# Layer 1 of a two-layer decoder trunk on one Trainium2 core: tokens 14 to 1039 in tiles of 256, down products of 512 columns in four banks, output stores of 128 rows

## The chip, the core and the metric

The kernel runs on one core of one Trainium2 chip as a single launch. The metric is device microseconds. Of the kernel before there are three timed runs, with a median of 3075.25 us (3072.14 to 3075.53), and one profiled execution.

## What is computed

The trunk has two layers. Sixteen learned meta tokens stand ahead of 1024 tokens of 1024 features (1040 in all); the meta tokens are dropped at the end. Layer 0 is a Mamba-2 mixer and a gated feed-forward network with a causal convolution of three taps; layer 1 is an attention over a shared K and V and such a network again. All is float32. The change lies in layer 1 behind the attention:

```python
h = h + o @ sb_w_o[j]                                    # o: (1040, 1024)
h = h + _conv_ffn(_rmsnorm(h, ffn_norm[1]), ffn_w_up[1], ffn_conv_w[1], ffn_conv_b[1], ffn_w_down[1])
return _rmsnorm(h, final_norm)[:, N_META:]               # the last 1024 rows

def _conv_ffn(u, w_up, conv_w, conv_b, w_down):
    h = _causal_dwconv(u @ w_up, conv_w, conv_b)         # 3 taps: a token needs the two ahead of it
    g, val = jnp.split(h, 2, axis=-1)                    # D_FF = 2816 each
    return (jax.nn.silu(g) * val) @ w_down
```

## The kernel before, in words

Data lie transposed: 128 features on the partitions, tokens in the columns, so the stream h is 8 tiles of 128 x 1040. Every large product is made of three float32r matmuls (`mm3`, L153 to L155): each operand is split into a high part (made by ScalarE, ACT) and the rest (made by VectorE, DVE, for activations and by GpSimd, POOL, for weights); high times high, high times low and low times high are summed in one PSUM bank. A bank holds 128 x 512 float32, and there are eight: `mm` 2, `sm` 3, `lg` 2, `ex` 1.

Behind the attention, both layers use the same functions, with token tiles of FN = 260 columns (four of them, 1040 in all):

- `o_proj` loads the attention's output by pairs of heads and the stream h, and adds the output projection to h in PSUM (`accumulate`: DVE adds the bank into h at L378). `enter_ffn` adds the last two or four pairs, makes the sums of squares (`square_row`, L794) and the RMS factors, stores h to DRAM (`hm`), and `forms` makes the operands of the up projection.
- `up` is the up projection as a fast 2 x 2 matrix product with seven products in place of eight, over two groups of two tiles. The matmuls are 262 columns wide (260 and the two ahead that the convolution needs): 3696 of them. DVE and ACT make the convolution; each result of 128 x 260 is stored to DRAM (`g`, L887).
- `down` is the down projection, a fast product with seven products (order 1, 7, 6, 5, 3, 4, 2), over the first 16 of 22 row blocks in two rounds. Each product of a round has two **halves** (sets x = 0 and 1 of rows), so there are 2 x 7 x 2 = 28 halves. `operands` makes a half's operands: differences of weights on POOL (L974 to L983), of activations on DVE (L975 to L985, 1040 columns), the splits on ACT (L989, L991), POOL (L990, `wl`) and DVE (L992, `gl`). A half has 48 matmuls of 260 columns: 4 row groups f, 2 tiles t of 260, 2 row blocks, 3 matmuls. A product's sum lives in eight banks, one for each (t, f): half 0 opens them, half 1 closes them, and `add` (L1035 on ACT, L1037 on DVE) brings each into its accumulator. The next product's first half can open a bank only when the add of this product's has emptied it. Then six row blocks are left, done directly (`accumulate`, 576 matmuls of 260 columns) for one token tile after the other, while DVE sums the seven products (`sums`, L1008).
- `finish` follows each tile of 348 tokens (348, 348, 344) as soon as its columns are done: the final norm, a transposition in chunks of 116 tokens (112 for the last) on TensorE (PE), the scaling, and stores of 116 rows of 4 KB (L1444). The third tile's 344 tokens come behind the last matmul. There the squares are taken from the transposed banks: ACT does L1430, DVE copies and squares (L1426, L1428), and the results are scaled by DVE (L1442) and by ACT and POOL together (L1439, L1440).

The queues of ACT, DVE, POOL, SP (DMA issue) and PE are in order. Outside of the mixer and the attention, the scheduler of the tile framework sets the order by its own estimate of times, so a change of shapes can reorder an engine's work. Up to the last instruction of the attention, the changed kernel has the same instructions in the same order on PE, DVE (but for one memset), ACT, POOL and SP.

Of the kernel before, what the change touches and what calls it, by code (L numbers as in the profile page):

```python
# [13 lines left out]
P = 128  # L14
D = 1024
# [14 lines left out]
FN = 260  # L30
HB = 2
FW = 264

# [33 lines left out]
class Trunk:  # L67
# [99 lines left out]
    def split_half(self, t, s):  # L167

        x = self.Q(s, F32R)
        hi, lo = x[:, : L // 2], x[:, QW // 2 : QW // 2 + L // 2]  # L170
# [200 lines left out]
    def accumulate(self, h, f, s0, n, w, ks, front=0, bank=None, base=0):  # L371

        ps = (bank or (self.ex if f % 3 == 2 else self.mm))("acc")
        c, o = slice(s0 - base, s0 - base + n), slice(front + s0, front + s0 + n)
# [328 lines left out]
    def out_proj(self, hd, ys, yd, pool):  # L703
# [3 lines left out]
        for g in range(3):  # L707
            ops = [self.split(ys[g][q] if yd[g] is None else self.fetch(yd[g][q], "y"), "y") for q in range(4)]
            for f in range(KD):
                w = self.load_w(a["w_out_f"][g, f], 4 * P)  # L710
                if g == 0:
                    h[f] = self.fetch(hd[f], "h", front=HB)
                for s0, n in TT:
                    self.accumulate(h, f, s0, n, lambda i, f: (w[0][:, i * P : i * P + P], w[1][:, i * P : i * P + P]), ops, HB)
        ops = [[self.split_half(ys[3][q][:, L // 2 * x : L // 2 * (x + 1)], "y") for q in range(4)] for x in range(2)]
        ws = [self.load_wd(a["w_out"][12 + i], pool if i < 2 else None) for i in range(4)]
        return self.enter_ffn(0, h, [(ws, o) for o in ops], pool)
# [4 lines left out]
    def enter_ffn(self, layer, h, last, pool):  # L722


        nc = self.nc
        r = self.rp.tile([P, QW], F32, tag="r", name=self.nm("r"))
        nc.gpsimd.tensor_copy(r[:, :HB], self.zero[:, :HB])
        d = self.dp.tile([KD, P, L], F32, tag=f"hm{layer}", name=f"hm{layer}")
# [3 lines left out]
        def tile(j, work):  # L732
            ws, ops = last[j // 2]
            ms[j] = self.sm("ms")
            for f in range(KD):
                self.accumulate(h, f, FN * j, FN, lambda i, f: (ws[i][0][:, f * P : f * P + P], ws[i][1][:, f * P : f * P + P]), ops, HB, next(banks), L // 2 * (j // 2))
                self.square_row(ms[j], h, j, f)
# [3 lines left out]
        def factors(j):  # L741

            c = r[:, HB + FN * j : HB + FN * j + FN]
            b, ps = self.tmp("y")[:, :FN], ms.pop(j)[:, :FN]
# [9 lines left out]
        def rest():  # L754
            forms.append(form_tiles())
            yield from self.forms(h, r, 1, f"ffn_norm{layer}", forms[1][1:], pool)

        def form_tiles():
# [3 lines left out]
            for x in wide[1]:  # L762
                nc.gpsimd.memset(x.bitcast(F32)[:, HB + 2 * FN : 2 * FW], 0.0)
            own = {i: (self.Q("bh", F32R), self.Q("bl", F32R)) for i in (0, 2, 3, 4, 6)}
            out = {i: [tuple(x[:, k * FW : k * FW + HB + FN] for x in own[i]) for k in range(KD // 2)] for i in own}
            both = [tuple(x[:, k % 2 * 2 * FW : k % 2 * 2 * FW + HB + 2 * FN] for x in wide[k // 2]) for k in range(KD // 2)]
            out[1] = [tuple(x[:, : HB + FN] for x in hl) for hl in both]
            out[5] = [tuple(x[:, FN :] for x in hl) for hl in both]
            return out, out, both

        def store(x):
            for k in range(KD):
                nc.sync.dma_start(d[k, :, L // 2 * x : L // 2 * (x + 1)], h[k][:, HB + L // 2 * x : HB + L // 2 * (x + 1)])
# [7 lines left out]
        work = self.forms(h, r, 0, f"ffn_norm{layer}", forms[0][1:], pool)  # L781
# [8 lines left out]
    def square_row(self, ms, h, j, f):  # L790

        q = self.tmp("sq")[:, :FN]
        self.nc.scalar.activation(q, h[f][:, HB + FN * j : HB + FN * j + FN], AF.Square)
        self.nc.tensor.matmul(ms[:, :FN], self.ones, q, start=f == 0, stop=f == KD - 1, skip_group_check=True)  # L794
# [5 lines left out]
    def forms(self, h, r, t, gain, tiles, pool):  # L800


        nc = self.nc
        N, N2 = HB + FN, HB + 2 * FN
        tt = nc.vector.tensor_tensor
        out, both = tiles
        s = slice(2 * FN * t, 2 * FN * t + N2)

        new = slice(s.start + HB * t, s.stop)
        for k in range(KD // 2):  # L810
# [8 lines left out]
            b11, b12, b21, b22 = b1[:, :N], b1[:, FN:], b2[:, :N], b2[:, FN:]  # L819
# [39 lines left out]
    def up(self, layer, w0, forms, rest, pool):  # L859

        nc = self.nc
        tt = nc.vector.tensor_tensor
        N = HB + FN
        cw, cb = f"ffn_conv_w{layer}", f"ffn_conv_b{layer}"
        d = self.dp.tile([KF, P, L], F32, tag=f"g{layer}", name=f"g{layer}")

        def block(b, t, w):
# [10 lines left out]
            def conv(x, i, c):  # L878
                o = self.tmp("c")
                self.conv(x, o[:, :FN], FN, 3, HB, lambda q: self.par(cw, (KF * i + b) * 3 + q), self.par(cb, KF * i + b))  # L880
                if i == 0:
                    nc.scalar.activation(o[:, :FN], o[:, :FN], AF.Silu)  # L882
                return o

            def done(g, v, j):
                self.last_up = tt(g[:, :FN], g[:, :FN], v[:, :FN], op=ALU.mult)  # L886
                nc.sync.dma_start(d[b, :, FN * j : FN * j + FN], g[:, :FN])  # L887
# [44 lines left out]
    def down(self, layer, gd, hd, pool, after):  # L932
# [3 lines left out]
        nc, a = self.nc, self.a  # L936
        H, S = D // 2, L // 2
# [94 lines left out]
        def add(i, f, t, ps, first):  # L1032
            x = acc[i, f][:, FN * t : FN * t + FN]
            if first and i in (1, 5, 6, 7):
                nc.scalar.activation(x, ps[:, :FN], AF.Copy)  # L1035
            else:
                tt(x, x, ps[:, :FN], op=ADD)  # L1037
# [35 lines left out]
        for m in range(0, len(plan), 2):  # L1073
# [3 lines left out]
            if r == 0 and i == 7:  # L1077
                for f in range(KD):
                    nc.sync.dma_start(h[f][:, :L] if f < 4 else h[f][:, half(0)], hd[f] if f < 4 else hd[f, :, half(0)])
# [5 lines left out]
            for x in range(2):  # L1085
# [446 lines left out]
```

## Time and profile before

| | |
|---|---|
| three timed runs, median | 3075.25 us |
| profiled execution, first to last instruction | 3077.5 us |
| attention's end, start of `o_proj` on PE | about 2207 us |
| up projection on PE | 2311.7 to 2785.9 us |
| 28 halves of the down products on PE | 2786.0 to 2975.2 us |
| six direct row blocks, with the finish of two tiles between | 2975.2 to 3051.9 us |
| from there to the end | 25.6 us |

The profiled execution is 2.25 us (0.07%) above the median of the runs. In the page, busy time is summed by engine; PE counts a matmul from its start to its modelled end, so matmuls overlap, and the pace is read from start to start. "PEld" is the loading of weights, which runs beside. A row of the view by lines or of the timeline has engine, source line, operation, output <- inputs, shapes and count; in brackets stands the idle time of the engine before it and what ended that.

### The profile page before, as it was taken

To read this page: it belongs to the slowest core of one execution; us is meant where nothing else is said; L and a number is where in the kernel's file an instruction comes from. 1 tells how busy PE (TensorE), PEld (TensorE's weight loads), DVE (VectorE), ACT (ScalarE), POOL (GpSimd) and SP (SyncE) were. 2 spreads that over 40 slices of the span, in tenths; PEclk is the share of its full clock that TensorE was granted. 3 is DMA by queue.
4 is the path that set the end of the run, shared out by engine and by line. 5 is a ranking of instruction groups with operands and counts; after the bars stand their busy time and mean duration, and the time that the engine had idled before them with its cause. 6 is when DMAs were issued, how large, how long until landed. Compare 5 with 4: busy or idle time off the path is not lost.

```text
span 3077.5 us, 58674 instructions
## 1 busy us (share of the span) xinstructions
PE 2897.7 (94%) x22535; PEld 2782.2 (90%) x22535; DVE 2336.0 (76%) x4030; ACT 1645.5 (53%) x3403; POOL 1411.6 (46%) x1289
## 2 busy tenths in 40 slices
PE   5999999989998999998999999999897999998997
PEld 2999898879988999998999999999797999998996
DVE  3576868885369888778966888888759888888874
ACT  2555545553245555654334888777635555554332
POOL 1154435452335666657733222222225666666741
PEclk8999999999999999999999999999998999999998
DMA  3333323323221222244132222221431222225221
GB/s 110 108 93 93 105 88 109 101 71 138 70 83 56 83 77 75 80 136 152 47 122 77 64 60 67 62 57 48 140 112 59 80 84 77 76 86 179 76 97 55
DMA packets 123220, 273.41 MB, mean 89 GB/s; under 512 B 13468, under 2 KB 53020, under 8 KB 122940
## 3 DMA queue, kind: packets, MB, share of 16 engines
q1 hardware_dynamic: 117622, 258.54, 26.9%
q10 hardware_dynamic: 4054, 6.56, 0.6%
q8 instruction: 177, 2.90, 0.4%
q0 software_dynamic: 1264, 4.57, 0.4%
q14 instruction: 103, 0.84, 0.1%
HBM read 201.25 MB, written 53.45 MB: 83 GB/s over the span
## 4 chain that ended last, share of the span: by engine, by line
PE 67%; DVE 17%; ACT 5%; issue 5%; DMA 3%; POOL 2%; ACTq 0%; POOLq 0%; SPq 0%; DVEq 0%
PE p L153 9%; PE p L154 9%; PE p L155 9%; PE acc L153 5%; PE acc L154 5%; PE acc L155 5%; PE pj L153 5%; PE pj L154 5%; PE pj L155 5%; DVE gl L992 3%; PE po L1297 2%; PE lg L1255 2%; DMA x<-in_x 1%; PE wT L1282 1%; DVE D L573 1%
## 5 line engine op out<-in xcount | busy, mean ns | idle before, releaser
L153 PE MATMUL pj<-uh,wh 128*128 128x348 f32 (+2 forms) x1536 | 507.0, 330 | 16.1 <-DVE qs L1206 7.2
L154 PE MATMUL pj<-ul,wh 128*128 128x348 f32 (+2 forms) x1536 | 497.3, 324 | 0.0
L155 PE MATMUL pj<-uh,wl 128*128 128x348 f32 (+2 forms) x1536 | 495.6, 323 | 0.0
L154 PE MATMUL p<-bl,fh 128*128 128x262 f32 x1408 | 400.9, 285 | 14.1 <-DVE bl L814 14.1
L153 PE MATMUL p<-bh,fh 128*128 128x262 f32 x1408 | 402.1, 286 | 2.5 <-ACT fh L845 1.4
L155 PE MATMUL p<-bh,fl 128*128 128x262 f32 x1408 | 400.1, 285 | 0.0
L846 POOL TENSOR_TENSOR fl<-x,fh 128x1024 fp32r<-128x1024 f32 x88 | 212.5, 2416 | 353.3 <-ACT fh L845 275.4
L147 POOL TENSOR_TENSOR wl<-w,wh 128x1024 fp32r<-128x1024 f32 (+2 forms) x80 | 163.9, 2051 | 351.8 <-ACT wh L146 351.7
L153 PEld LDWEIGHTS pj<-uh,wh 128*128 128x128 f32 x1536 | 291.8, 190 | 23.7 <-DVE qs L1206 9.2
L154 PE MATMUL p<-bl,wh 128*128 128x262 f32 x1056 | 303.1, 287 | 8.7 <-DVE bl L814 8.7
L153 PE MATMUL p<-bh,wh 128*128 128x262 f32 x1056 | 302.3, 287 | 6.2 <-ACT bh L813 6.2
L155 PE MATMUL p<-bh,wl 128*128 128x262 f32 x1056 | 301.2, 286 | 0.0
L154 PEld LDWEIGHTS pj<-ul,wh 128*128 128x128 f32 x1536 | 292.0, 190 | 1.2 <-issue 0.5
L155 PEld LDWEIGHTS pj<-uh,wl 128*128 128x128 f32 x1536 | 291.4, 190 | 0.5 <-issue 0.2
L278 DVE SCALAR_TENSOR_TENSOR c<-p,params,c 128x260 f32<-128x260 f32 x528 | 251.4, 484 | 47.2 <-ACT c L275 37.5
L153 PE MATMUL acc<-gh,wh 128*128 128x260 f32 x896 | 262.1, 293 | 22.9 <-DVE p L1037 10.7
L154 PEld LDWEIGHTS p<-bl,fh 128*128 128x128 f32 x1408 | 267.2, 190 | 16.3 <-DVE bl L814 16.0
L153 PEld LDWEIGHTS p<-bh,fh 128*128 128x128 f32 x1408 | 266.8, 190 | 5.2 <-ACT bh L813 2.0
L154 PE MATMUL acc<-gl,wh 128*128 128x260 f32 x896 | 260.3, 291 | 9.8 <-DVE gl L992 9.5
L155 PEld LDWEIGHTS p<-bh,fl 128*128 128x128 f32 x1408 | 266.6, 190 | 0.1
L886 DVE TENSOR_TENSOR c<-c,c 128x260 f32<-128x260 f32 x176 | 255.7, 1453 | 7.5 <-ACT c L882 4.5
L155 PE MATMUL acc<-gh,wl 128*128 128x260 f32 x896 | 259.0, 290 | 1.2 <-POOL wl L990 1.2
(311 smaller groups left out, 8566.7 us busy)
## 6 DMA issues: line engine op xcount, KB each, us to landing
w<-in_w_up SPq DMA_DIRECT2D x88, 512.0 KB
g<-c SPq DMA_DIRECT2D x176, 130.0 KB
w<-in_w_down SPq DMA_DIRECT2D x44, 512.0 KB
w<-in_w_in SPq DMA_DIRECT2D x40, 512.0 KB
b<-g SPq DMA_DIRECT2D x32, 520.0 KB
E<-ea_d SPq DMA_DIRECT2D x32, 464.0 KB
D<-acs_d SPq DMA_DIRECT2D x32, 420.5 KB
h<-h_d SPq DMA_DIRECT2D x16, 520.0 KB
```

The costliest lines, as they stand in the source:

```text
L147: nc.gpsimd.tensor_tensor(wl[:, :n], w32[:, :n], wh[:, :n].bitcast(F32), op=ALU.subtract)
L153: mm(out, wh, uh, start=first, stop=False, skip_group_check=joins)
L154: mm(out, wh, ul, start=False, stop=False, skip_group_check=joins)
L155: mm(out, wl, uh, start=False, stop=last, skip_group_check=joins)
L278: nc.vector.scalar_tensor_tensor(out, ps[:, o + i : o + i + n], wcol(i), out, op0=ALU.mult, op1=ALU.add)
L573: nc.vector.tensor_scalar(dk[:, i], dk[:, i], self.cols[:n, 1, cc, h0 + i : h0 + i + 1], 0.0, op0=ALU.subtract, op1=ALU.min)
L846: tt(lo[:, :n], t, hi[:, :n].bitcast(F32), op=ALU.subtract)
L886: self.last_up = tt(g[:, :FN], g[:, :FN], v[:, :FN], op=ALU.mult)
L992: tt(gl, x, gh.bitcast(F32), op=SUB)
L1255: nc.tensor.matmul(ps[:nt, :m], part[:, c0 : c0 + nt], ks[a][:, s0 : s0 + m], start=x == 0, stop=x == 1)
L1282: nc.tensor.transpose(pt[:ns, x * CB : x * CB + nt], bt[a][:nt, x * CB : x * CB + ns], self.ident[:nt, :nt])
L1297: nc.tensor.matmul(po[64 * a : 64 * a + 64, w], v[: CH[c][1], c, 64 * a : 64 * a + 64], wt[a][: CH[c][1], c, :nt], start=x == 0, stop=x == ...
```

## The change

For layer 1 alone (FNS = 260 for layer 0, 256 for layer 1), and without any change in what layer 0 does:

- h is loaded from token 14 on (ORG = META - HB = 14): 1026 columns, two for the convolution and 1024 for the output. Tiles are 256 wide, the first of `o_proj` 258; the up matmuls are 258 wide, and all the DVE, ACT and DMA work of a tile shrinks from 260 to 256 columns.
- In `down` a half's columns are S = 512. Since that fits a bank, `parts` is one part of 512 columns: a half is 24 matmuls of 512 columns (4 f, 2 row blocks, 3 matmuls) into four banks, with adds of 512 columns. `kinds` becomes a cycle over eight banks, so that consecutive products take different fours.
- `finish` works on four tiles of 256 tokens in chunks of 128: two tiles behind the second direct tile, one behind the third, and one, the last, behind the fourth. Stores are of 128 rows; for the last tile they go out in halves of 512 columns, and all of its scaling is on DVE (L1466 of the changed kernel) in place of DVE, ACT and POOL.

```diff
-FN = 260
+FNS = (260, 256)
 HB = 2
+ORG = META - HB
...
     def enter_ffn(self, layer, h, last, pool):
-        nc = self.nc
+        nc, F = self.nc, FNS[layer]
...
+        edges = [0] + [HB + F * j for j in range(1, 5)]
+        if layer == 0:
+            edges[0] = HB
+            nc.gpsimd.tensor_copy(r[:, :HB], self.zero[:, :HB])
+        tiles = [(x, y - x) for x, y in zip(edges, edges[1:])]
...
     def down(self, layer, gd, hd, pool, after):
-        H, S = D // 2, L // 2
+        H, S = D // 2, 2 * F
+        parts = [(0, S)] if S <= 512 else [(0, F), (F, F)]
...
-        kinds = (self.mm, self.sm, self.lg, self.sm, self.mm, self.sm, self.lg, self.ex)
+        kinds = cycle((self.mm, self.sm, self.lg, self.sm, self.mm, self.sm, self.lg, self.ex))
...
+            o, n = parts[t]
             for q in range(2):
-                c, e = slice(q * H + f * P, q * H + f * P + P), slice(FN * t, FN * t + FN)
-                self.mm3(ps[:, :FN], wh[:, c], wl[:, c], gh[:, q, e], gl[:, q, e], first and q == 0, not first and q == 1)
+                c, e = slice(q * H + f * P, q * H + f * P + P), slice(o, o + n)
+                self.mm3(ps[:, :n], wh[:, c], wl[:, c], gh[:, q, e], gl[:, q, e], first and q == 0, not first and q == 1)
...
-                tt(x, x, ps[:, :FN], op=ADD)
+                tt(x, x, ps[:, :n], op=ADD)
...
-                for n, (t, f) in enumerate((t, f) for t in range(2) for f in range(4)):
+                for t, f in ((t, f) for t in range(len(parts)) for f in range(4)):
                     if x == 0:
-                        ps[t, f] = kinds[n]("acc")
+                        ps[t, f] = next(kinds)("acc")
                     part(ps[t, f], made[m + x], f, t, x == 0)
...
     def o_proj(self, hd, od, pool):
...
-            h[f] = self.fetch(hd[f], "h", front=HB)
+            h[f] = self.Q("h")
+            self.nc.sync.dma_start(h[f][:, : L - ORG], hd[f, :, ORG:])
             for j in range(4):
-                self.accumulate(h, f, FN * j, FN, lambda i, f: (w[0][:, i * P : i * P + P], w[1][:, i * P : i * P + P]), ops[j // 2], HB)
+                o, e = (HB + F * j) * (j > 0), HB + F * (j + 1)
+                self.accumulate(h, f, o, e - o, lambda i, f: (w[0][:, i * P : i * P + P], w[1][:, i * P : i * P + P]), ops[j // 2])
...
     def finish(self, h, j):
+        for i in ((0, 1), (2,), (3,))[j]:
+            self.finish_tile(h, i)
+
+    def finish_tile(self, h, j):
...
-        s0, n = TT[j]
-        chunks = [(i, *CH[3 * j + i]) for i in range(3)]
+        n = FNS[1]
+        s0, last = n * j, j == 3
+        chunks = [(i, s0 + P * i) for i in range(n // P)]
...
-                if b and i < 2:
-                    nc.scalar.activation(y[:m, w], p[:m], AF.Copy, scale=r[:m, i : i + 1])
-                    nc.gpsimd.tensor_tensor(y[:m, w], y[:m, w], self.gfin[:m, w], op=ALU.mult)
+                if b and not last:
+                    nc.scalar.activation(y[:, w], p, AF.Copy, scale=r[:, i : i + 1])
+                    nc.gpsimd.tensor_tensor(y[:, w], y[:, w], self.gfin[:, w], op=ALU.mult)
                 else:
-                    nc.vector.scalar_tensor_tensor(y[:m, w], p[:m], r[:m, i : i + 1], self.gfin[:m, w], op0=ALU.mult, op1=ALU.mult)
-            s = META if t0 == 0 else 0
-            nc.sync.dma_start(out[t0 + s - META : t0 + m - META, :], y[s:m, :])
+                    nc.vector.scalar_tensor_tensor(y[:, w], p, r[:, i : i + 1], self.gfin[:, w], op0=ALU.mult, op1=ALU.mult)
+                if last:
+                    nc.sync.dma_start(out[t0 : t0 + P, w], y[:, w])
+            if not last:
+                nc.sync.dma_start(out[t0 : t0 + P, :], y)
```

How this moves instructions is shown at three places. First DVE in the second round of the down products, from the low split of product 6's first half (`gl`, L992, L1001 in the changed kernel) to the last add of product 7 (`p` is its accumulator, `acc` the banks, `b` the activations); before:

```order
L992 TENSOR_TENSOR gl_34608<-b_33803,gh_34607 128x2x520
L985 TENSOR_TENSOR b_33803<-b_34219,b_33803 128x2x520
L1037 TENSOR_TENSOR p_33447<-p_33447,acc_34549 128x260
L1037 TENSOR_TENSOR p_33447<-p_33447,acc_34556 128x260
L992 TENSOR_TENSOR gl_34674<-b_33873,gh_34673 128x2x520
L1037 TENSOR_TENSOR p_33448<-p_33448,acc_34563 128x260
L1037 TENSOR_TENSOR p_33448<-p_33448,acc_34570 128x260
L985 TENSOR_TENSOR b_33873<-b_34287,b_33873 128x2x520
L1037 TENSOR_TENSOR p_33447<-p_33447,acc_34577 128x260
L1037 TENSOR_TENSOR p_33447<-p_33447,acc_34584 128x260
L1037 TENSOR_TENSOR p_33448<-p_33448,acc_34591 128x260
L1037 TENSOR_TENSOR p_33448<-p_33448,acc_34598 128x260
```

and now:

```order
L1001 TENSOR_TENSOR gl_34123<-b_33654,gh_34122 128x2x512
L994 TENSOR_TENSOR b_33654<-b_33902,b_33654 128x2x512
L1048 TENSOR_TENSOR p_33438<-p_33438,acc_34092 128x512
L1001 TENSOR_TENSOR gl_34161<-b_33696,gh_34160 128x2x512
L1048 TENSOR_TENSOR p_33438<-p_33438,acc_34099 128x512
L994 TENSOR_TENSOR b_33696<-b_33942,b_33696 128x2x512
L1048 TENSOR_TENSOR p_33439<-p_33439,acc_34106 128x512
L1048 TENSOR_TENSOR p_33439<-p_33439,acc_34113 128x512
```

Among the same operand steps (2 x 520 or 2 x 512 columns) stood eight adds of 260 columns from eight banks; four adds of 512 columns stand there now.

Second, POOL at the same place, from the weights' low part `wl` of product 7's first half to that of product 5's first half; before:

```order
L990 TENSOR_TENSOR wl_34478<-w_33944,wh_34477 128x1024
L977 TENSOR_TENSOR w_33944<-w_34082,w_33944 128x1024
L980 TENSOR_TENSOR w_33805<-w_33805,w_33944 128x1024
L990 TENSOR_TENSOR wl_34544<-w_34013,wh_34543 128x1024
L977 TENSOR_TENSOR w_34013<-w_34151,w_34013 128x1024
L990 TENSOR_TENSOR wl_34610<-w_33944,wh_34609 128x1024
L980 TENSOR_TENSOR w_33875<-w_33875,w_34013 128x1024
L983 TENSOR_TENSOR w_33944<-w_34217,w_33944 128x1024
L990 TENSOR_TENSOR wl_34676<-w_34013,wh_34675 128x1024
L983 TENSOR_TENSOR w_34013<-w_34285,w_34013 128x1024
L990 TENSOR_TENSOR wl_34742<-w_33805,wh_34741 128x1024
```

and now:

```order
L999 TENSOR_TENSOR wl_34049<-w_33739,wh_34048 128x1024
L986 TENSOR_TENSOR w_33739<-w_33821,w_33739 128x1024
L989 TENSOR_TENSOR w_33656<-w_33656,w_33739 128x1024
L999 TENSOR_TENSOR wl_34087<-w_33780,wh_34086 128x1024
L986 TENSOR_TENSOR w_33780<-w_33862,w_33780 128x1024
L999 TENSOR_TENSOR wl_34125<-w_33739,wh_34124 128x1024
L989 TENSOR_TENSOR w_33698<-w_33698,w_33780 128x1024
L992 TENSOR_TENSOR w_33739<-w_33900,w_33739 128x1024
L999 TENSOR_TENSOR wl_34163<-w_33780,wh_34162 128x1024
L999 TENSOR_TENSOR wl_34201<-w_33656,wh_34200 128x1024
L992 TENSOR_TENSOR w_33780<-w_33940,w_33780 128x1024
```

The shapes are the same. One difference of weights for product 3 (L983, now L992), which stood between the last two `wl`, has moved behind them.

Third, SP's last issues, the stores of the output; before:

```order
L1444 DMA out<-y_35794 100x1024
L1444 DMA out<-y_35824 116x1024
L1444 DMA out<-y_35809 116x1024
L1444 DMA out<-y_36043 116x1024
L1444 DMA out<-y_36073 116x1024
L1444 DMA out<-y_36058 116x1024
L1444 DMA out<-y_36309 116x1024
L1444 DMA out<-y_36319 112x1024
L1444 DMA out<-y_36314 116x1024
```

and now:

```order
L1470 DMA out<-y_34999 128x1024
L1470 DMA out<-y_35014 128x1024
L1470 DMA out<-y_35068 128x1024
L1470 DMA out<-y_35083 128x1024
L1470 DMA out<-y_35301 128x1024
L1470 DMA out<-y_35316 128x1024
L1468 DMA out<-y_35536 128x512 x2
L1468 DMA out<-y_35541 128x512 x2
```

Nine stores of 100 to 116 rows became six of 128 full rows and four of 128 half rows; behind the last matmul come the last three of before and the last four of now.

More of the change, by code (lines that the diff above doesn't have):

```diff
@@ L741, in factors @@
         def factors(j):
[L743 to L744 removed]
+            o, n = tiles[j]
+            c = r[:, o : o + n]
+            b, ps = self.tmp("y")[:, :n], ms.pop(j)[:, :n]
             if j % 2 == 0:
@@ L1434, in finish @@
+            nc.vector.tensor_tensor(ss[:, :2], s2[:, 0], s2[:, 1], op=ALU.add)
+            r = self.token_rstd(ss, P, 2)
+        for i, t0 in chunks:
             y = self.Q("y")[:, :D]
```

135 lines of the change are left out of this document (69 added, 66 removed).

## The prediction, before the changed kernel was run

> **What bounds the kernel now.** I read the page first, then the part behind the attention by stages (the changed kernel has the same program up to there), then the pace of matmuls by width, the waits of the down products, and the end. The stages are cut at 2834.4, 2881.1 and 2918.5 us where halves 6, 14 and 20 of the down products start on PE (counted by 48 matmuls from 2786.0):
>
> ```profile
> span 3077.5 us, 58674 instructions
> PE 67%; DVE 17%; ACT 5%; issue 5%; DMA 3%; POOL 2%; ACTq 0%; POOLq 0%; SPq 0%; DVEq 0%
> ```
>
> ```profile
> core 0: us, PE busy (x) PEld busy (x) DVE busy (x) ACT busy (x) POOL busy (x), PEclk, DMA share, GB/s
> 2203.00:2311.70 108.70, 108.50 (x857) 105.68 (x858) 58.64 (x131) 42.04 (x87) 26.71 (x19) 0.98 0.36 123
> 2311.70:2786.00 474.30, 458.46 (x3713) 454.33 (x3712) 396.86 (x633) 273.02 (x565) 304.08 (x173) 0.98 0.26 86
> 2786.00:2834.40 48.40, 39.68 (x291) 38.45 (x289) 45.27 (x22) 22.48 (x39) 41.06 (x14) 0.89 0.31 110
> 2834.40:2881.10 46.70, 46.53 (x384) 46.12 (x385) 32.91 (x33) 18.36 (x25) 27.27 (x11) 1.00 0.52 171
> 2881.10:2918.50 37.40, 35.05 (x291) 34.63 (x290) 36.19 (x34) 13.11 (x13) 35.82 (x12) 1.00 0.00 1
> 2918.50:2975.20 56.70, 51.35 (x386) 50.52 (x385) 43.24 (x64) 21.24 (x24) 32.42 (x12) 0.91 0.37 122
> 2975.20:3051.90 76.70, 76.70 (x650) 76.70 (x649) 39.94 (x84) 17.34 (x31) 11.59 (x9) 1.00 0.14 45
> 3051.90:3077.50 25.60, 3.00 (x26) 2.51 (x24) 7.95 (x20) 5.09 (x11) 3.05 (x2) 0.66 0.24 75
> ```
>
> PE sets the output projection, the up projection, halves 6 to 13 and the direct blocks: it is busy all through. In halves 0 to 5 and 14 to 19 DVE and POOL are both busy nearly without a gap, and PE is not. In halves 20 to 27 nobody is full: PE waits, and its clock (0.91) falls. The last 25.6 us hold almost no work.
>
> **Pace by width.** Operands and weights change with every matmul, so PE runs at a fixed step for each width. The timeline of PE has two runs without a break, 478 matmuls of 260 columns between the first pair of rows and 68 of 348 between the second (the rows that end them are the next instruction's):
>
> ```profile
> 2215.21 0.28 PE L154 MATMUL acc<-ol,wh 128*128 128x260 f32 x1
> 2272.56 0.38 PE L794 MATMUL ms<-sq,ones 128*128 128x260 f32 x1
> ...
> 1656.87 0.32 PE L153 MATMUL pj<-uh,wh 128*128 128x348 f32 x1
> 1667.65 0.32 PE L155 MATMUL pj<-uh,wl 128*128 128x348 f32 x1
> ```
>
> 57.35 us / 478 is 120.0 ns, 10.78 / 68 is 158.5 ns: 0.44 ns for each column. By that line 256 columns take 118.2, 258 take 119.1 against 120.9 for 262, and 512 columns 230.9; I take 230. No float32r matmul wider than 352 is in the trace, so this is bounded. Above: in proportion to 260 columns, 236 ns. Below: plain float32 matmuls of 512 columns, whose two records stand 1.02 - 0.59 = 0.43 us apart in the rows here (timeline, and the view of the tile S); if a record is two passes, one pass is 215 ns.
>
> ```profile
> 165.97 1.02 PE L619 MATMUL S<-xde,bk 116*128 116x512 f32 x2
> ```
>
> ```profile
> L619 PE MATMUL S<-xde,bk x64: 589/592/697, 166.0 to 674.0; 116*128 116x512 f32 x64
> L626 DVE TENSOR_TENSOR state<-state,S x28: 668/677/690, 182.9 to 681.4; 128x512 f32<-128x512 f32 x28
> ```
>
> The Trainium skill, "TensorE: Matmul & The Clock Gate", section "Back-to-back issue gap", gives the isolated gap as columns / 2.4 + 2.5 ns. At 260 columns that would be 110.8, and the trace has 120.0, so it does not hold here; at 512 it says 215.8, and by it the sum below would be 16 x 24 x 14.2 ns = 5.5 us better.
>
> **The waits of the down products.** PE's groups in 2786.0 to 2975.2:
>
> ```profile
> L153 PE MATMUL acc<-gh,wh 128*128 128x260 f32 x448 | 131.2, 293 | 10.9 <-DVE p L1037 5.3 <-DVE c L278 3.1 <-DVE h L1037 2.4
> L154 PE MATMUL acc<-gl,wh 128*128 128x260 f32 x448 | 130.5, 291 | 4.9 <-DVE gl L992 4.8
> L155 PE MATMUL acc<-gh,wl 128*128 128x260 f32 x448 | 130.0, 291 | 0.8 <-POOL wl L990 0.8
> ```
>
> 7.7 us are waits for a bank that DVE had still to empty (L1037), 4.8 for `gl`. A wait costs more than itself. Behind one of these waits, at 2928, the step is
>
> ```profile
> 2928.57 0.42 PE L154 MATMUL acc<-gl,wh 128*128 128x260 f32 x1
> 2928.79 0.42 PE L155 MATMUL acc<-gh,wl 128*128 128x260 f32 x1
> ```
>
> 0.22 us in place of 0.12: half clock, which the stage's 0.91 reflects. The adds are late because DVE's other work is slow, as its timeline and POOL's show:
>
> ```profile
> 2804.19 3.43 DVE L978 TENSOR_TENSOR b<-b,b 128x1040 f32<-128x1040 f32 x1
> 2857.79 1.23 DVE L992 TENSOR_TENSOR gl<-b,gh 128x1040 fp32r<-128x1040 f32 x1
> 2895.88 1.42 DVE L1037 TENSOR_TENSOR p<-p,acc 128x260 f32<-128x260 f32 x4
> ...
> 2882.36 2.40 POOL L990 TENSOR_TENSOR wl<-w,wh 128x1024 fp32r<-128x1024 f32 x1 [3.32 <-ACT wh L989]
> 2884.84 3.29 POOL L977 TENSOR_TENSOR w<-w,w 128x1024 f32<-128x1024 f32 x1
> 2914.96 6.76 POOL L990 TENSOR_TENSOR wl<-w,wh 128x1024 fp32r<-128x1024 f32 x2
> ```
>
> The same DVE step takes 1.2 us alone and 3.4 while POOL works, and POOL's goes from 2.4 to 3.3: about 1.2 + 2.2, they take turns. An add out of a bank (1.42 / 4, overlapping starts) stays at 0.35 to 0.42 in the midst of it. So a wider add is cheap, but operands cannot come faster than one DVE and one POOL step in 3.35 us.
>
> **The change part by part** (gains in us, against the profiled 3077.5).
>
> *Narrower tiles ahead of the products.* Output projection: 768 matmuls x 1.7 ns = 1.3, at least 0 if loads set it. Up projection: 3696 x 1.8 ns = 6.5; PE waits only at its start, on DVE, whose work shrinks by 1.5% too. Least 4, if DVE sets more of it. The shorter DMAs (1024 bytes in place of 1040) are hidden by PE; DMA is 26% busy in the up stage.
>
> *Halves 0 to 5* (48.4): the turns of DVE and POOL set them. Faster matmuls and free banks only lengthen the waits for `gl`; 12 DVE steps lose 16 columns each, some 0.02 us apiece: 0.3. Bounds -2 (longer waits at half clock) and +3 (if the 3.1 us wait on L278, for banks of the up projection, turned out to count).
>
> *Halves 6 to 13* (46.7): 8 x 24 x 230 ns = 44.2, gain 2.5.
>
> *Halves 14 to 19* (37.4): the bank waits fall away, and POOL's queue is next; already now the `wl` of half 20 ends at 2914.96 + 3.38 = 2918.3, just as that half starts (2918.5). POOL ends the `wl` of half 16 at 2884.8, 3.7 after half 14 starts, and then needs nine steps of 3.35 (the rows of the order) up to half 20's. PE alone would need 6 x 5.52 = 33.1. Half 19 comes eight steps behind: 3.7 + 8 x 3.35 = 30.5 after half 14, where PE would be ready at 27.6. A wait of 2.9, plus 1.5 to 2 for half clock, leaves half 20 at about 37.4. Gain 0; bounds -2 and +4.3.
>
> *Halves 20 to 27* (56.7): waits of 5 us and half clock here come from banks. With the other four banks free, an add may be late by a whole product. The adds cost DVE 4 x 0.68 (the 512-column row of tile S) in place of 8 x 0.42 for each product, so DVE's 43 us become some 40, under PE's 8 x 5.52 = 44.2. I take 45.2 for what is left of waits: gain 11.5, bounds 6 and 12.5.
>
> *Direct blocks* (76.7): 576 x 1.8 ns = 1.0. The finish between has 48 transpositions as before.
>
> *The end* (25.6). Its rows, of PE, DVE, POOL and SP, and then the DMA by windows:
>
> ```profile
> 3051.78 0.28 PE L155 MATMUL acc<-g,wl 128*128 128x260 f32 x1
> 3051.91 2.34 PE L1405 MATMUL fin<-ident,h 128*116 128x128 f32 x20
> ...
> 3053.81 0.69 DVE L1426 COPY copy<-fin 116x512 f32<-116x512 f32 x1 [1.28 <-PE fin L1405]
> ...
> 3059.42 2.07 DVE L1442 SCALAR_TENSOR_TENSOR y<-fin,ty,gfin 116x512 f32<-116x512 f32 x3
> ...
> 3060.22 3.05 POOL L1440 TENSOR_TENSOR y<-y,gfin 116x512 f32<-116x512 f32 x2 [16.07 <-ACT y L1439]
> ...
> 3061.52 3.57 SPq L1444 DMA_DIRECT2D out<-y  x3
> ```
>
> ```profile
> 3070.00:3072.00 2.00, 0.00 (x0) 0.00 (x0) 0.00 (x0) 0.00 (x0) 0.00 (x0) 0.50 0.25 98
> 3074.00:3076.00 2.00, 0.00 (x0) 0.00 (x0) 0.00 (x0) 0.00 (x0) 0.00 (x0) 0.50 0.14 59
> ```
>
> From 3070 to 3072 a quarter (0.25) of the 16 DMA engines work, later less: the stores of 116 rows lie on few of them, and bytes still flow to about 3076, 11 us behind the end of the last issue (3061.52 + 3.57 = 3065.1). A 128-row store of 2080-byte rows in the earlier stage behaves otherwise:
>
> ```profile
> 2309.29 0.32 SPq L773 DMA_DIRECT2D hm<-h  x1
> ```
>
> ```profile
> 2310.40:2310.80 0.40, 0.40 (x6) 0.40 (x5) 0.40 (x2) 0.40 (x1) 0.00 (x0) 1.00 0.96 369
> 2310.80:2311.20 0.40, 0.40 (x6) 0.40 (x5) 0.40 (x2) 0.40 (x1) 0.00 (x0) 1.00 0.23 67
> ```
>
> All engines carry it, and it is through 1.6 us after its issue. So now, with the last matmul at 0: the add and 12 transpositions of 2.34 / 20 = 0.12 us to 1.7; two copies and two squares on DVE, 4 x 0.69 (one of three takes 2.07 / 3), to 4.5; the factors to 6.0 (today six such steps from 3053.81 end near 3057.95, and the first scaling is at 3059.42); four scalings of 0.69 to 8.7, with a store behind each; the last of them through 1.6 + 0.3 later, at 10.6; and the 1.5 us that today lie between 3076 and the end at 3077.5: 12 in place of 25.7. Gain 13.7, bounds 9 (a store that takes some 5 us more) and 15.
>
> *Sum:* 1.3 + 6.5 + 0.3 + 2.5 + 0 + 11.5 + 1.0 + 13.7 = 36.8; 3077.5 becomes 3040.7. The profile lies 2.25 above the median of the runs, so against 3075.25 I expect 3038.5.
>
> **The rivals.** *Operands bind everywhere:* once banks never stop PE, the turns of DVE and POOL set halves 6 to 27 too, and the gain of 2.5 + 11.5 shrinks to about 5. For it: both engines are full in two of four stretches, and a wait for a bank can turn into one for `gl` of like length, so that only the half clock and the width bring something. Against: in halves 20 to 27 neither DVE (43.2 of 56.7) nor POOL (32.4) is full. Time 3040.7 + 9 - 2.25 = 3047.5. The Trainium skill, "SBUF — State Buffer", section "SBUF: two separate sides", calls the port pair of DVE and GpSimd an exclusive lock that its holder keeps for a whole instruction while the other blocks; the 3.4 us rows agree, and by that rule wider adds out of PSUM cost the operands nothing.
>
> *PE binds everywhere:* no wait on POOL in halves 14 to 19 (+4.3) and the lower width bound in part (+3). Time 3031.
>
> *The landing does not shorten:* if a store to the output costs its 10 us whatever its rows are, the end gains only what its arithmetic gains, 3 or 4. Against: the row above. Time 3048.5.
>
> *512 columns are slow:* the one mechanism that ends on the other side. At two steps of 260, 240 ns, the change still gains about 34: 23 outside the halves and 11 from waits. So from 240 + 34 / 0.672 = 291 ns for each of the 672 matmuls on, the kernel is slower; at 430 ns, two records of tile S a matmul, 672 x 0.19 = 128 less 34 makes some 3170. The width line and the S rows speak against it. That the change doesn't do what it says can be left out: the order shows four adds of 512 columns for a half pair, and stores of 128 rows.
>
> **How the numbers follow.** Forecast 0.58, operands bind 0.16, PE binds 0.14, landing 0.08, slow columns 0.04. The first four are all faster by far more than 0.2% (6 us), about what a measurement of this kernel tells from no change: faster 0.95, same 0.01, slower 0.04. The predicted time is the forecast's, 3038. The terms' bounds, which hardly all fall on one side, give 3028 to 3051, and this holds the first four cases: 3027 to 3051.
>
> **What would show it.** The step of 512-column matmuls: 230 ns. No wait of PE on an add in the halves; in its place waits on `wl` in halves 19 and 20. The stage from the first half to the last 174 to 175 us in place of 189.2, the up projection 467 to 468 in place of 474.3. Behind the last matmul 12 us, with all DMA engines busy for each store. The prediction is wrong if PE's step at 512 lies above 240, if DVE's adds or `gl` hold halves 20 to 27, or if the last landing comes more than 3 us after its issue.

## The result, and the profile after

The changed kernel takes 3054.09 us (median of four runs, 3051.92 to 3055.15) against 3074.73 for the kernel before in the runs taken with it: a ratio of 0.9939 (95% interval 0.9925 to 0.9953), 20.6 us faster. The forecast was 3038, with a range of 3027 to 3051.

The profiled execution has a span of 3050.2 us (3051.92 as a run), 27.3 below that of before. Not all of this is the change: the output projection, up to which both kernels have the same instructions, starts at 2202.40 in this execution and at 2206.92 in that of before, and between 2202.1 and 2207.9 in all ten profiled executions of this study. So stages are compared from there on, and then the change is worth 22.8 us in the profiles. The windows of the changed kernel, cut at the first matmul of each stage (output projection, up projection, halves 0 to 5, 6 to 13, 14 to 19, 20 to 27, direct blocks, end):

```profile
span 3050.2 us, 57256 instructions
```

```profile
2202.40:2305.82 103.42, 103.27 (x821) 101.39 (x819) 56.50 (x127) 40.06 (x83) 26.57 (x19) 0.99 0.37 128
2305.82:2777.03 471.21, 456.19 (x3712) 452.53 (x3711) 395.37 (x632) 269.19 (x563) 305.69 (x173) 0.98 0.26 85
2777.03:2826.55 49.52, 40.62 (x146) 31.05 (x145) 46.22 (x24) 18.68 (x25) 41.80 (x14) 0.83 0.37 133
2826.55:2871.05 44.50, 44.50 (x194) 36.06 (x192) 28.80 (x23) 20.25 (x25) 28.48 (x11) 1.00 0.46 154
2871.05:2906.64 35.59, 33.67 (x145) 26.97 (x144) 34.34 (x23) 13.01 (x13) 34.21 (x11) 1.00 0.03 6
2906.64:2953.09 46.45, 45.77 (x193) 35.65 (x192) 45.05 (x36) 19.20 (x22) 30.67 (x12) 1.00 0.34 111
2953.09:3038.60 85.51, 79.71 (x649) 79.10 (x648) 53.17 (x101) 22.63 (x46) 18.67 (x15) 0.96 0.17 68
3038.60:3050.20 11.60, 1.91 (x18) 1.67 (x16) 6.64 (x17) 3.07 (x7) 0.00 (x0) 0.71 0.24 90
```

The columns are length, busy time of PE, PEld, DVE, ACT and POOL, granted clock, DMA share and GB/s. The sixth row is full on PE (45.77 of 46.45), as forecast, but full on DVE too (45.05), which was not. The seventh row, where PE was busy without a break before (76.70 of 76.70), now has holes. Stage by stage, each from its first matmul to the next stage's first (the end from the last matmul):

| stage | before | after | gain | forecast |
|---|---|---|---|---|
| output projection | 104.8 | 103.4 | 1.4 | 1.3 |
| up projection | 474.3 | 471.2 | 3.1 | 6.5 |
| halves 0 to 5 | 47.5 | 49.5 | -2.0 | 0.3 |
| halves 6 to 13 | 47.6 | 44.5 | 3.1 | 2.5 |
| halves 14 to 19 | 37.4 | 35.6 | 1.8 | 0 |
| halves 20 to 27 | 56.8 | 46.5 | 10.3 | 11.5 |
| direct blocks | 76.6 | 85.4 | -8.8 | 1.0 |
| end | 25.7 | 11.7 | 14.0 | 13.7 |
| sum | 870.6 | 847.8 | 22.8 | 36.8 |

One row makes most of the difference to the forecast: the direct blocks lost 8.8. PE's groups there, and PE's timeline at their start:

```profile
L156 PE MATMUL acc<-g,wl 128*128 128x256 f32 x128 | 36.6, 288 | 2.0 <-POOL wl L1057 2.0
L154 PE MATMUL acc<-g,fh 128*128 128x256 f32 x64 | 19.0, 297 | 3.8 <-DVE h L1048 3.8
```

```profile
2956.97 0.38 PE L156 MATMUL acc<-g,wl 128*128 128x256 f32 x1 [2.05 <-POOL wl L1057]
2958.72 0.58 PE L154 MATMUL acc<-g,fh 128*128 128x256 f32 x1 [1.36 <-DVE h L1048]
2959.10 0.42 PE L155 MATMUL acc<-g,fh 128*128 128x256 f32 x1
2959.32 0.42 PE L156 MATMUL acc<-g,fl 128*128 128x256 f32 x1
...
2964.91 0.49 PE L154 MATMUL acc<-g,fh 128*128 128x256 f32 x1 [2.39 <-DVE h L1048]
```

Three waits make 5.8 us: one for the weights' low part from POOL, two for banks that DVE has still to empty into h (L1048, the last product's adds). Behind them PE steps by some 0.215 us for a while. The 64 matmuls up to 2970.0, which at 0.118 would take 7.5 us, take 16.9: 9.4 more, 5.8 of waits and 3.6 of half pace, and narrower tiles save some of it again. DVE's timeline shows why the adds are late:

```profile
2952.43 2.28 DVE L1018 TENSOR_TENSOR h<-h,p 128x512 f32<-128x512 f32 x1
2954.63 0.68 DVE L1048 TENSOR_TENSOR h<-h,acc 128x512 f32<-128x512 f32 x1
2955.23 2.84 DVE L1018 TENSOR_TENSOR h<-h,p 128x512 f32<-128x512 f32 x2
2957.99 0.67 DVE L1048 TENSOR_TENSOR h<-h,acc 128x512 f32<-128x512 f32 x1
2958.70 2.55 DVE L1018 TENSOR_TENSOR h<-h,p 128x512 f32<-128x512 f32 x1
...
2964.18 0.67 DVE L1048 TENSOR_TENSOR h<-h,acc 128x512 f32<-128x512 f32 x1
```

PE left the last product at 2953.1; DVE starts that product's last add at 2964.2, 11 us later. It works without a gap, and between the adds stand the sums of the seven products (L1018), each up to 2.55 us while POOL makes weights. In the kernel before, PE left the last product at 2975.2, and DVE started the last add 0.7 us later:

```profile
2975.94 0.42 DVE L1037 TENSOR_TENSOR h<-h,acc 128x260 f32<-128x260 f32 x1
```

### The profile page after: what moved, and what is told of

Its sections match the earlier page's. It is cut to its first block, busy times and chain, and to the rows that moved or that the text cites. A ratio compares the mean times of both kernels' runs of the same rounds, so it can differ in the third digit from the quotient of the medians.

```text
span 3050.2 us, 57256 instructions
## 1 busy us (share of the span) xinstructions
PE 2883.7 (95%) x21855; PEld 2737.1 (90%) x21855; DVE 2345.9 (77%) x3994; ACT 1642.3 (54%) x3396; POOL 1414.2 (46%) x1282
## 4 chain that ended last, share of the span: by engine, by line
PE 69%; DVE 16%; ACT 5%; issue 5%; DMA 3%; POOL 2%; SPq 0%; DVEq 0%; ACTq 0%; POOLq 0%
PE p L154 9%; PE p L155 9%; PE p L156 9%; PE acc L155 6%; PE acc L154 6%; PE acc L156 6%; PE pj L154 5%; PE pj L155 5%; PE pj L156 5%; PE po L1308 2%; DVE gl L1001 2%; PE lg L1266 1%; DVE kp L1279 1%; DMA x<-in_x 1%; PE wT L1293 1%
## 5 line engine op out<-in xcount | busy, mean ns | idle before, releaser
L155 PE MATMUL p<-bl,fh 128*128 128x262 f32 (+1 forms) x1408 | 401.0, 285 | 14.0 <-DVE bl L822 14.0
L154 PE MATMUL p<-bh,fh 128*128 128x262 f32 (+1 forms) x1408 | 401.5, 286 | 2.2 <-ACT fh L853 1.4
L156 PE MATMUL p<-bh,fl 128*128 128x262 f32 (+1 forms) x1408 | 399.2, 285 | 0.0
L155 PE MATMUL p<-bl,wh 128*128 128x262 f32 (+1 forms) x1056 | 301.9, 286 | 8.5 <-DVE bl L822 8.5
L154 PE MATMUL p<-bh,wh 128*128 128x262 f32 (+1 forms) x1056 | 301.8, 287 | 6.1 <-ACT bh L821 6.1
L156 PE MATMUL p<-bh,wl 128*128 128x262 f32 (+1 forms) x1056 | 300.8, 285 | 0.0
L279 DVE SCALAR_TENSOR_TENSOR c<-p,params,c 128x260 f32<-128x260 f32 (+1 forms) x528 | 250.2, 482 | 45.5 <-ACT c L276 35.3
L894 DVE TENSOR_TENSOR c<-c,c 128x260 f32<-128x260 f32 (+1 forms) x176 | 253.2, 1439 | 6.8 <-ACT c L890 3.8
L899 ACT ACTIVATE ft<-p 128x262 f32<-128x262 f32 (+1 forms) x352 | 126.6, 383 | 204.7 <-DVE p L902 185.8
L154 PE MATMUL acc<-gh,wh 128*128 128x260 f32 (+1 forms) x672 | 219.0, 330 | 14.5 <-DVE p L1048 5.4
```

The costliest lines, as they stand in the source:

```text
L154: mm(out, wh, uh, start=first, stop=False, skip_group_check=joins)
L155: mm(out, wh, ul, start=False, stop=False, skip_group_check=joins)
L156: mm(out, wl, uh, start=False, stop=last, skip_group_check=joins)
L279: nc.vector.scalar_tensor_tensor(out, ps[:, o + i : o + i + n], wcol(i), out, op0=ALU.mult, op1=ALU.add)
L894: self.last_up = tt(g[:, :F], g[:, :F], v[:, :F], op=ALU.mult)
L899: nc.scalar.activation(s[:, :N], ps[:, :N], AF.Copy)
```

## The experiments

The theory: DVE's work around halves 20 to 27 is a fixed load. Before, PE waited for it inside the halves; with a second set of banks PE runs on and meets the same load at the direct blocks. The rivals: the order of banks alone, or the narrower tiles and the new finish. Each run's stages are read as in the table; "from the output projection on" is the row "sum".

**The down part undone.**

```diff
-        parts = [(0, S)] if S <= 512 else [(0, F), (F, F)]
+        parts = [(0, F), (F, F)]
```

> The changed kernel, with the down products again in two parts of 256 columns and eight banks a product; tiles of 256, stores of 128 rows and the last tile's scaling stay. The question is whether the 8.8 us that the six direct blocks lost (85.4 from the first to the last of their 576 matmuls, 76.6 before) belong to the wide products. Exposed work (the wide products end some 10 us earlier, and DVE and POOL are not done with what the direct blocks need): the halves go back to about 187, the direct blocks to 76 to 77, and the whole is only 2 to 4 us slower than the changed kernel, near 3057. Rival, the narrower tiles or the new finish cost the direct blocks their time: the halves go back to 187, the direct blocks stay near 85, and the whole is 11 slower, near 3065.

Measured: ratio 0.9938 (0.9926 to 0.9951). Its halves 20 to 27 and direct blocks:

```profile
2911.85:2968.22 56.37, 50.21 (x387) 49.39 (x385) 42.31 (x64) 20.89 (x24) 33.42 (x12) 0.91 0.35 113
2968.22:3044.30 76.08, 76.08 (x650) 76.08 (x649) 42.88 (x92) 21.48 (x44) 15.23 (x13) 1.00 0.15 57
```

The halves are back at 188.1 in all, the direct blocks are full on PE again, and from the output projection on it takes 850.5, 2.7 more than the changed kernel. So the loss belongs to the wide products; they gained 12.0 in the halves and gave back 9.4 behind them. By the medians the two kernels can't be told apart.

**Only the order of banks.** The first direct tile takes its banks in the products' order, and from the second tile on as before.

```diff
-        banks = cycle((self.mm, self.mm, self.ex, self.lg, self.lg))
+        banks = kinds if layer else cycle((self.mm, self.mm, self.ex, self.lg, self.lg))
...
+            if j == 1 and layer:
+                banks = cycle((self.mm, self.mm, self.ex, self.lg, self.lg))
```

> The changed kernel, with the first direct tile's eight sums in the order of banks of the products, so that the first four are the banks of the product before the last, long empty, and the last product's four come after them. Bank order (the direct tile asks too early for the last product's banks): the two waits on the last adds (3.8 us) and the half clock behind them go, the direct blocks take 79 to 80 in place of 85.4, and the whole is 5 to 6 faster. Late DVE (DVE is some 10 us behind at that point, whatever the banks): the waits move to the fifth sum or to the operands, the direct blocks take 83 to 86, and the whole is within 2 of the changed kernel.

Measured: 0.9912 (0.9899 to 0.9925), direct blocks 79.9, 5.5 less. The groups of PE there keep one wait:

```profile
L156 PE MATMUL acc<-g,wl 128*128 128x256 f32 x128 | 36.2, 284 | 2.0 <-POOL wl L1057 2.0
```

So the bank rival's number came out, and my theory's did not: DVE is as late as before (45.09 us busy of 46.61 in halves 20 to 27), but PE no longer asks for the banks that wait for it. Lateness and order together make 5.5 of the 9.4 us lost. The other 3.9 (79.9 against 76.0 with parts of 256 columns) hold the wait for POOL's late `wl`, 2.0, and half pace behind it (clock 0.98), which the order of banks leaves as they are.

**The sums moved away.** Each of the 28 sums is tied behind the add of a direct block.

```diff
-                        tt(acc[x, f], acc[x, f], acc[y, f], op=ADD)
+                        late(tt(acc[x, f], acc[x, f], acc[y, f], op=ADD))
...
-                self.accumulate(out, f, F * j, ...
-                for _ in range(2 if j == 0 else 1):
+                behind[0] = self.accumulate(out, f, F * j, ...
+                for _ in range((1, 2, 1, 1)[j] if layer else 2 if j == 0 else 1):
```

`late` makes the sum follow `behind[0]` on DVE, in layer 1 alone. Since lines were put in, L1018, L1048 and L1068 of the changed kernel are L1025, L1055 and L1075 here; L1075 makes the low parts of the direct blocks' activations.

> The changed kernel, with the 28 sums of the seven products (DVE, 128 x 512 each) tied behind the direct blocks' adds, one sum for each add of the first tile and two for each of the second, so that none stands between the last products' operands and adds. Late DVE: the adds of the last product follow PE at once, the waits at the start of the direct blocks fall away in most part, also POOL's steps there shrink from 2.65 to 2.4, the direct blocks take 77 to 79 in place of 85.4, and the whole is 6 to 8 faster, near 3047. Bank order: nothing of this, within 2 of the changed kernel, or slower by some us if the sums then hold the second tile or the finish.

Measured: 3043.9 us, 0.9899 (0.9887 to 0.9912). Its halves 20 to 27 and direct blocks, and its DVE as the products end:

```profile
2908.54:2953.05 44.51, 44.51 (x194) 36.04 (x193) 31.12 (x28) 19.63 (x23) 31.94 (x12) 1.00 0.39 132
2953.05:3029.50 76.45, 76.45 (x649) 76.45 (x648) 51.56 (x108) 22.23 (x46) 16.28 (x14) 1.00 0.16 62
```

```profile
2953.41 0.95 DVE L1075 TENSOR_TENSOR g<-g 128x512 fp32r<-128x512 f32 x1 [2.44 <-ACT g L1074]
2954.28 0.68 DVE L1055 TENSOR_TENSOR h<-h,acc 128x512 f32<-128x512 f32 x1
...
2955.48 1.27 DVE L1055 TENSOR_TENSOR h<-h,acc 128x512 f32<-128x512 f32 x2
```

Both stages are full on PE. DVE's load in the halves falls from 45 to 31 us, it even waits, and the last add is done by 2956.8 in place of 2964.9. All waits in these two stages went, POOL's too, though the banks are asked for in the changed kernel's order, and the direct blocks take 76.3, less than the 77 to 79 expected. By its median this is the fastest of the complete versions here: 30 us under the kernel before, and its interval lies below that of the changed kernel.

**The sums moved away, with eight banks and 256 columns.** The edits of the first and the third run together.

> Down products in two parts of 256 columns and eight banks, as in the run with such parts, and in addition the 28 sums tied behind the direct blocks' adds. If what held PE in halves 20 to 27 before (56.4 to 56.8 us) was that DVE's sums stood between the adds, so that banks came late, then halves 20 to 27 take 46 to 48 also with eight banks and 256 columns, the whole from the output projection on is some 7 to 10 shorter than with such parts alone (850.5), near 842, and the wide products are worth no more than some 4 to 5 beside it (837.6 with both). Rival, the wait is one of banks as such (no second set, one add late holds the next product): halves 20 to 27 stay above 52.

Measured: 0.9912 (0.9898 to 0.9927); halves 20 to 27 49.9, direct blocks 76.1, 844.3 from the output projection on:

```profile
2914.57:2964.44 49.87, 46.37 (x386) 45.53 (x385) 32.19 (x48) 20.68 (x24) 30.99 (x12) 1.00 0.40 127
```

The halves lie between the two expectations (46 to 48, above 52). With parts of 256 columns these halves lost 11 us to waits and to the half pace behind them (56.4 against some 45.3 for 384 matmuls of 0.118). 6.5 of these were due to sums between the adds; with eight banks 3.5 us of waits for banks remain. With the sums out of the way the wide products are worth 6.8 in the profiles (844.3 less 837.6), not 2.7, and more than the 4 to 5 that were expected at most.

**The width without the second set.** Wide products, but each in the same four banks.

```diff
                         ps[t, f] = next(kinds)("acc")
+                        if layer and f == 3:
+                            [next(kinds)("skip") for _ in range(4)]
```

> The changed kernel with the wide products, but every product of layer 1 in the same four banks (the other four are passed over). If the second set of banks is what freed halves 20 to 27, they go from 46.4 to 52 to 57, with waits on the adds (L1048) as before the change. If the width alone did it (half as many, cheaper adds a product), halves 20 to 27 stay at 46 to 48. The direct blocks, whose first banks change too, are not read from this run.

Measured: 0.9928 (0.9915 to 0.9941). PE's groups of halves 20 to 27 and the two stages:

```profile
L154 PE MATMUL acc<-gh,wh 128*128 128x512 f32 x64 | 26.2, 409 | 8.4 <-DVE h L1048 6.7 <-DVE p L1048 1.7
```

```profile
2907.30:2962.20 54.90, 46.52 (x193) 37.00 (x192) 47.94 (x41) 21.18 (x24) 33.97 (x13) 0.94 0.37 121
2962.20:3038.50 76.30, 76.30 (x649) 76.27 (x648) 47.29 (x96) 21.49 (x44) 14.87 (x13) 1.00 0.15 56
```

54.9: the second set did free the halves, as forecast. But the two stages together take 131.2, against 131.8 in the changed kernel (46.45 + 85.39): what the second set gained in the halves (8.5) was lost again behind it (9.1). (The direct blocks' first banks differ too, as the expectation says; their sum is still telling, since PE is full there.)

**POOL's load cut.** The differences and sums of weights on POOL are left out, so that the products get other weights.

```diff
-                    pt(a21, a11, a21, op=SUB)
+                    pw(a21, a11, a21, op=SUB)
```

(so in four places; `pw` does nothing in layer 1)

> The changed kernel without POOL's sixteen differences and sums of weights in layer 1 (so the products get other weights; this part of the computation is left out). Turn-taking of DVE and POOL sets halves 0 to 5 and 14 to 19: with POOL's load there more than halved, DVE's steps are 1.2 in place of 3.4 more often, halves 0 to 5 take 36 to 41 in place of 44.8 to 49.5, halves 14 to 19 go from 35.6 to PE's 33.3, and the start of the direct blocks hardly changes. Rival, DVE's own queue or the loads set halves 0 to 5: 44 or more.

Measured: 0.9867 (0.9852 to 0.9881). Its halves 0 to 5, 6 to 13 and 14 to 19, and two equal DVE steps in the first of them:

```profile
2776.90:2813.52 36.62, 33.65 (x147) 26.96 (x146) 32.44 (x20) 19.56 (x27) 18.96 (x7) 1.00 0.43 156
2813.52:2858.06 44.54, 44.54 (x194) 36.06 (x193) 27.89 (x22) 18.73 (x22) 19.34 (x8) 1.00 0.45 153
2858.06:2891.46 33.40, 33.40 (x146) 27.05 (x145) 29.38 (x25) 13.78 (x14) 14.52 (x6) 1.00 0.05 17
```

```profile
2802.02 1.22 DVE L995 TENSOR_TENSOR b<-b,b 128x1024 f32<-128x1024 f32 x1
...
2805.14 3.32 DVE L995 TENSOR_TENSOR b<-b,b 128x1024 f32<-128x1024 f32 x1
```

Halves 0 to 5 take 36.6, DVE's busy time there falls from 46 to 32 us with its instructions in the same order (a low split takes 1.74 us in the mean, and 3.39 in the changed kernel), and halves 14 to 19 are full on PE. The direct blocks, which I expected hardly to change, take 82.0: the wait for POOL is gone there, the two waits for DVE's adds are still 3.8. So POOL's load sets both stretches. In halves 0 to 5 it does so through the turns with DVE; in halves 14 to 19 this run can't part the turns from the mere length of POOL's queue. The Trainium skill, "SBUF — State Buffer", section "Who interferes with whom", says that a `tensor_tensor` with both inputs in SBUF contends with GpSimd's reads; the 1.22 and 3.32 us agree, and so does the 0.67 us of the adds, whose second input is in PSUM.

**The stores of the last tile cut into 116 and 12 rows.**

```diff
-                    nc.sync.dma_start(out[t0 : t0 + P, w], y[:, w])
+                    nc.sync.dma_start(out[t0 : t0 + 116, w], y[:116, w])
+                    nc.sync.dma_start(out[t0 + 116 : t0 + P, w], y[116:, w])
```

> The changed kernel, with each of the last four stores cut into one of 116 rows and one of 12. Rows set the landing (a store of 116 rows lies on few DMA engines): the time from the last matmul of the direct blocks to the end goes from 11.7 to some 18 to 21. Rival, arithmetic (the end got shorter since DVE alone scales, ahead of fewer and earlier stores): 12 to 13.5, the price of four more issues.

Measured: 0.9962 (0.9949 to 0.9975); the end takes 21.6 us in place of 11.7. The windows of the end, first of the changed kernel, then of this one:

```profile
3045.00:3047.00 2.00, 0.00 (x0) 0.00 (x0) 2.00 (x4) 0.00 (x0) 0.00 (x0) 0.50 0.45 174
3047.00:3049.00 2.00, 0.00 (x0) 0.00 (x0) 0.18 (x1) 0.00 (x0) 0.00 (x0) 0.50 0.93 350
```

```profile
3049.00:3053.00 4.00, 0.00 (x0) 0.00 (x0) 0.00 (x0) 0.00 (x0) 0.00 (x0) 0.50 0.46 94
3053.00:3057.00 4.00, 0.00 (x0) 0.00 (x0) 0.00 (x0) 0.00 (x0) 0.00 (x0) 0.50 0.34 99
3057.00:3060.70 3.70, 0.00 (x0) 0.00 (x0) 0.00 (x0) 0.00 (x0) 0.00 (x0) 0.50 0.09 34
```

With 128 rows 0.93 of the DMA engines work and move 350 GB/s; the same bytes in stores of 116 and 12 rows go at 94 to 99. The last issue ends 12.5 us behind the last matmul, with four stores 9.1; from there to the end it is 9.1 against 2.7. So 6.5 of the 9.9 us are the landing and 3.4 the issues, twice as many and longer each. The four issues of the changed kernel:

```profile
3045.23 2.31 SPq L1468 DMA_DIRECT2D out<-y  x4
```

In the kernel before, the last issue ended 13.3 us behind the last matmul, and 12.4 more followed to the end. So of the gain of 14.0, some 9.7 lie behind the last issue and the rest ahead of it.

**The last tile scaled by three engines.**

```diff
-                if b and not last:
+                if b:
```

(with the copied bank as ACT's input for the last tile)

> The changed kernel, with the second halves of the last tile's rows scaled by ACT and POOL, as the other tiles' are, in place of DVE; stores of 128 rows stay. Two DVE steps of 0.7 go (1.3), an ACT step of 0.7 and a POOL step of 1.3 to 1.5 for each chunk run beside them. If the store's shape alone made the end short, the time from the last matmul to the end is 11.7 within 1: two POOL steps end 0.7 + 2 x 1.4 behind the factors against 2.7 for four DVE steps, so 12 to 13. If scaling on DVE alone was a part of the gain of 14, it is 14 or more.

Measured: the end takes 12.2, the whole 0.993 (0.9918 to 0.9943). The end is within 1 of 11.7, as expected if the shape of the stores made it short; scaling on DVE alone is worth some 0.5 us. What makes up the gain ahead of the last issue (a last tile of 256 tokens in place of 344 among it) was not taken apart.

## Why the prediction was wrong

*Direct blocks, "576 x 1.8 ns = 1.0".* This step failed. The term counts matmuls and their step alone. It puts waits in this stage at nothing, and gives no reason but PE's full row of before. That row was full because PE came late: while it stood waiting in halves 20 to 27, DVE emptied the last banks and POOL made weights for the direct blocks, so that the last add began 0.7 us behind PE's last product. Once the wait there went, it began 11 us behind it. The stage lost 8.8 in place of a gain of 1.0: 5.8 of waits and 3.6 of half pace, less what the narrower matmuls saved (0.6, by the run with parts of 256 columns: 76.0 against 76.6). The prediction's own numbers held the warning: by them DVE was to have some 40 us of work under PE's 44.2, which left it some 4 us to catch up.

*Halves 20 to 27.* The size came out (10.3 for 11.5), the reason only in part, so that there is luck in it. DVE's load did not fall to 40 but rose from 43.3 to 45.1, in a shorter stretch: the adds there took 9.2 us for 14.5, but the steps with both inputs in SBUF took longer, beside a POOL that is busy for 30.7 of 46.5 us in place of 32.5 of 56.8, as these groups of before and after show:

```profile
L992 DVE TENSOR_TENSOR gl<-b,gh 128x1040 fp32r<-128x1040 f32 x6 | 9.6, 1593 | 4.6 <-PE acc L154 4.6
```

```profile
L1001 DVE TENSOR_TENSOR gl<-b,gh 128x1024 fp32r<-128x1024 f32 x6 | 11.1, 1854 | 0.0
```

The second set of banks hid this lateness for the length of the halves, no longer. Halves 20 to 27 and direct blocks together take 133.3 us before, 132.3 with 256 columns, 131.2 with the same four banks and 131.8 in the changed kernel: with the sums in DVE's way and this order of banks, the wide products gained 0.5 there.

*Up projection, 6.5.* A mis-sized term: 3.1. The prediction put 0.44 ns on each column. The timelines of PE (before, then after) have 2000 matmuls between the rows of each pair:

```profile
2519.58 0.28 PE L153 MATMUL p<-bh,wh 128*128 128x262 f32 x1
2762.18 0.29 PE L155 MATMUL p<-bh,fl 128*128 128x262 f32 x1
```

```profile
2512.64 0.29 PE L154 MATMUL p<-bh,wh 128*128 128x258 f32 x1
2753.43 0.28 PE L156 MATMUL p<-bh,fl 128*128 128x258 f32 x1
```

121.3 and 120.4 ns: 0.9 for four columns, not 1.8. 258 columns are dearer than the line says (119.1), which the output projection of the changed kernel shows by itself, with 66 matmuls of 256 columns between its first two rows and 18 of 258 between the last two:

```profile
2246.05 0.28 PE L154 MATMUL acc<-oh,wh 128*128 128x256 f32 x1
2253.84 0.28 PE L154 MATMUL acc<-oh,wh 128*128 128x258 f32 x1
2256.01 0.28 PE L154 MATMUL acc<-oh,wh 128*128 128x256 f32 x1
```

118.0 and 120.6 ns. Why two more columns cost 2.6 ns was not tried.

*Halves 0 to 5.* The loss of 2.0 can't be put down to the change: in five kernels that have the same instructions in the same order here (the changed one, and those with other direct banks, the same four banks, 116 rows, three engines) this part took 49.5, 47.0, 46.4, 44.8 and 48.8, and 47.5 in the one profile of before. That DVE and POOL set it was right.

*Halves 6 to 13, 14 to 19.* Right in kind. The prediction cut half 6 at 2834.4; counted by 48 matmuls a half it starts at 2833.5, and the term would have been 3.4 in place of 2.5 (measured 3.1). The wide step is 231.8 ns, for 230 forecast: 288 matmuls from half 7's first to half 19's first.

```profile
2832.11 0.40 PE L154 MATMUL acc<-gh,wh 128*128 128x512 f32 x1
2898.88 0.40 PE L154 MATMUL acc<-gh,wh 128*128 128x512 f32 x1
```

In half 19 PE waits 1.9 us for POOL's `wl`, for 2.9 worked out, and the 1.5 to 2 for half clock behind it did not come (granted clock 1.00), so the stretch gained 1.8. In the kernel with the sums moved away the same wait of 1.9 us was followed by half pace (0.43 us a step in place of 0.23, clock 0.95), and the stretch took 37.2. Why it came there and not here is open.

*The end.* Right in time (11.7 for 12), and in cause for the 9.7 us behind the last issue.

*The rivals.* "Operands bind everywhere" had the engine and came nearer in time (3047.5), but by luck: it put the place inside the halves, where it did not bind. The landing did shorten, to 2.7 us behind the last issue, and the slow columns did not come. No rival looked past the stage that was freed, and none of the three things that the prediction named as showing it wrong came: the step stayed below 240 ns, no add and no `gl` held halves 20 to 27, and the landing took less than 3 us.

## What to carry to other kernels

When a wait goes, follow the engine that was waited for beyond the stage: its work is still there, and if it has no slack, the next stage pays. Here a second set of banks by itself only shifted such a wait; taking work out of the late engine's queue there (28 sums that nobody needed yet) removed it, 10 us for a few lines, and only then was the second set, with the wide matmuls, worth 6.8 us. Cost a stage that is "full on one engine" with the question of what runs ahead of it, and why it could.

## What the hardware showed that was not expected

- The step of a float32r matmul with its weight load is not a straight line in its width: 118.0 ns at 256 columns, 120.6 at 258, 120.0 at 260, 121.3 at 262, 231.8 at 512. The Trainium skill, "TensorE: Matmul & The Clock Gate", section "Back-to-back issue gap", gives the isolated gap as columns / 2.4 + 2.5 ns, an estimate of 109.2 and 215.8 ns at 256 and 512; the trace has 8% and 7% more.
- With the same instructions in the same order, the stretch in which DVE and POOL take turns took 44.8 to 49.5 us from kernel to kernel, and the attention ended anywhere within 5.8 us. Stages, not ends, had to be compared.
- Stores of 116 and 12 rows moved 94 to 99 GB/s, stores of 128 rows 350.
